# A gated short-convolution layer on one core: sharing buffers between small weight pieces, turning all tokens at the start, and a new load order

## The chip, the core and the metric

The kernel runs on one core of one Trainium2 chip. The metric is the device time of one execution in microseconds (us), which is to be small. The core has four compute engines that run side by side: PE (TensorE, matrix products), DVE (VectorE), ACT (ScalarE) and POOL (GpSimd, hardly used here). SP (SyncE) only issues DMA transfers. Each engine works through its own list of instructions in order; an instruction waits until the semaphores that it names have been reached, and everything behind it on the same engine waits with it.

## What is computed

With 256 tokens of width 2048 and a branch width of 4096, in float32:

```python
h = rmsnorm(x, norm_g)                              # (256, 2048)
mod = silu(c) @ ada_w + ada_b                       # (3 * 2048): shift, scale, gate
h = h * (1 + scale) + shift
b_gate, c_gate, v, g = split(h @ w_in, 4)           # w_in (2048, 16384)
u = causal_depthwise_conv(c_gate * v, conv_w)       # width 3
y = (b_gate * u * silu(g)) @ w_out                  # w_out (4096, 2048)
out = rmsnorm(x + gate * y, final_g)
```

## The kernel before

**Precision.** Each float32 weight tile is split into two parts that PE can take at full rate: ACT casts it to `hi` (L318), DVE subtracts to get `lo` (L323). The modulated tokens are kept turned (channels on the partitions) as `hT`, also in two parts: ACT writes the high part (L310), DVE recomputes the value in `xs` (L311) and writes the low part (L314). Three products replace one: high by high, high weight by low token, low weight by high token. A chunk of 128 channels `k` against 512 columns takes 12 products of 128x256 (`chunk_products`, in that order for each of four column blocks).

**Stages.** (1) The front: load x (four 512 KB pieces) and the shift and scale columns of `ada_w` for channels k = 0 and 1, sum them against silu(c), normalise and turn part of the tokens, form `hT` for k = 0, 1. (2) The stage with tiles `mm_s`: the first half of the columns of `w_in` as 16 parts of 512 columns (4 "chapters" `ch` by 4 quarters `q`). Not all channels of `hT` exist yet, so `plan()` first runs all 16 parts over the few k that are ready, and then comes back to each part as more groups of two k are ready. Sums wait in `acc` tiles. The parts of the plan that matter here are 13 parts over k = 0, 1; three parts over k = 0 to 3; five over k = 2, 3; and then one over k = 2 to 5, the first that uses k = 4. (3) The stage `mm_b`: the second half of the columns, all k at once. (4) `mm_o`: the product with `w_out`, the gate, the last norm.

**ada groups.** The shift and scale for the next two k come from eight pieces of 512 KB (`at`, two loads of 256 KB each, four buffers). DVE multiplies and adds them into `gv` (L410 for the first row block, L412 for the rest). `ada_done` then turns `gv` on PE (`tp_g`, L419), sums over rows on DVE (`gs`, L420), adds the bias (`mod`, L307) and calls `modulate`.

**Order.** A scheduler orders the instructions of each engine by priority and by a simulated time line; the front is pinned to the written order. All loads of weights go through SP's one queue, in order. There are three buffers each for the loaded piece (`raw`), for `hi` and for `lo`, of 2048 columns; a piece over k = 0, 1 fills only half of one. A load waits until DVE has read the buffer's last piece, `hi` and `lo` until PE has. Idle products (`idle`, L243) keep PE busy in the front. The tokens of k = 0 to 3 are scaled and turned in the front (`turn_x`, L287 to L299), those of k = 4 to 15 in three portions after the 4th, 7th and 10th part (`LATER`); `conv_w` is loaded at the start and turned after the 4th part.

Of the kernel before, what the change touches and what calls it, by code (L numbers as in the profile page):

```python
# [8 lines left out]
F32 = mybir.dt.float32  # L9
F32R = mybir.dt.float32r  # L10
AF = mybir.ActivationFunctionType
# [106 lines left out]
def short_conv_layer(ctx: ExitStack, tc: tile.TileContext, x, c, norm_g, ada_w, ada_b, w_in, conv_w, w_out, final_g, out):  # L118
# [73 lines left out]
    xt = [[slot([P, HX], f"x{t}{dh}") for dh in range(2)] for t in range(TT)]  # L192
    for t in range(TT):
        for dh in range(2):
            nc.sync.dma_start(xt[t][dh], x[t * P : (t + 1) * P, dh * HX : (dh + 1) * HX])
    nc.scalar.dma_start(rows1[64:80, :], c.rearrange("o (k p) -> (o k) p", p=P))
# [9 lines left out]
    for n, (j, kk) in enumerate(((0, 4), (4, 4), (8, 4), (12, 2), (14, 1), (15, 1))):  # L206
        at = wpool.tile([P, SLOT], F32, tag=("lo", "hi")[n % 2], name="at0", bufs=3)[:, : kk * 2 * NK0 * P]
        at = at.rearrange("p (k s f) -> p k s f", k=kk, s=2)
        if n == 0:
            wpool.tile([P, 32], F32, tag="line3", name="line3", bufs=1)  # L210
        if j == KT - 1:
            raw0 = raw_tile("raw0")
            first_load(raw0, 0)
        for s in range(2):
            nc.sync.dma_start(at[:, :, s, :], adas[:, j : j + kk, s, 0 : NK0 * P])  # L215
        first_ada.extend(at[:, i] for i in range(kk))
    for k in range(1, NK0):
        first_load(raw0, k)

    ident = const.tile([P, P], F32, tag="ident", name="ident")  # L220
# [15 lines left out]
        return tp  # L236


    tp_idle = psum.tile([P, CT, T], F32, tag="mm", name="tp_idle")

    def idle(n):
        for _ in range(n):
            nc.tensor.transpose(tp_idle[:, 0, 0:P], ident, ident)  # L243


    warm = const.tile([P, 1], F32, tag="warm", name="warm")
    silu = nc.scalar.activation(silu_c, turn(rows1, 64, 80, None), AF.Silu)
    root = nc.scalar.activation(warm, eps_t, AF.Sqrt)
    tc.add_manual_dep(root.ins, silu.ins.name, after, reason="one change of table")
    idle(IDLE[0])  # L250
# [3 lines left out]
    idle(IDLE[1])  # L254


    ssq = const.tile([P, 2, TT], F32, tag="ssq", name="ssq")
# [22 lines left out]
    hl_ = hT[:, :, T : 2 * T]  # L280
    xs = [slot([P, CT, T], f"xs{j}") for j in range(KT // CT)]

    def turn_x(k0, k1, vector=False):

        c0, n = k0 % 8 * P, (k1 - k0) * P
        x0, x1 = (xt[t][k0 // 8][:, c0 : c0 + n] for t in range(TT))
        nc.scalar.activation(x0, x0, AF.Copy, scale=rstd[:, 0:1])  # L287
        if vector:
            nc.vector.tensor_scalar_mul(x1, x1, rstd[:, 1:2])
        else:  # L290
            nc.scalar.activation(x1, x1, AF.Copy, scale=rstd[:, 1:2])
        for i in range(0, k1 - k0, 2):
            tp = psum.tile([P, 2, T], F32, tag="sm", name="tp_x", bufs=2)
            for j in range(2):
                for t, xn in enumerate((x0, x1)):
                    nc.tensor.transpose(tp[:, j, t * P : (t + 1) * P], xn[:, (i + j) * P : (i + j + 1) * P], ident)
            for j in range(2):
                k = k0 + i + j
                nc.scalar.activation(xs[k // CT][:, k % CT], tp[:, j], AF.Copy, scale=gT[:, k : k + 1])  # L299

    mod = const.tile([P, 2, KT], F32, tag="mod", name="mod")

# [10 lines left out]
            )  # L313
            nc.vector.tensor_tensor(out=hl_[:, k], in0=hf, in1=hh_[:, k].bitcast(F32), op=ALU.subtract)  # L314

    def split_hi(raw, n):
        hi = wpool.tile([P, SLOT], F32R, tag="hi", name="hi", bufs=3)
        nc.scalar.copy(hi[:, :n], raw[:, :n])  # L318
        return hi

    def split_lo(raw, n, hi, lo_tag="lo"):
        lo = wpool.tile([P, SLOT], F32R, tag=lo_tag, name="lo", bufs=3)
        nc.vector.tensor_tensor(out=lo[:, :n], in0=raw[:, :n], in1=hi[:, :n].bitcast(F32), op=ALU.subtract)  # L323
        return hi, lo

    def split(raw, n, lo_tag="lo"):

        return split_lo(raw, n, split_hi(raw, n), lo_tag)
# [2 lines left out]

    sums0 = psum.tile([P, 512], F32, tag="sm", name="sum0", bufs=2)
    gv0 = adap.tile([P, 2, 2 * P], F32, tag="gv", name="gv0")[:, :, 0 : NK0 * P]
    turn_x(0, 4)

    def sum0(k, rows, col, halves=(0, 1)):


        for o in range(2 * NK0):
            if o // NK0 in halves:  # L340
                nc.tensor.matmul(
                    sums0[:, o * P : (o + 1) * P], rows[:, o // NK0, (o % NK0) * P : (o % NK0 + 1) * P],
                    col.to_broadcast([P, P]),
                    start=k == min(IDLE_AT) and o == 0, stop=k is None, skip_group_check=True,
                )

    for k in range(KT):
        c_k = silu_c[:, k : k + 1]
        at, gv = first_ada[k], gv0
        if k in IDLE_AT:  # L350
            idle(IDLE_AT[k])
# [13 lines left out]
    idle(IDLE_END)  # L365
    pinned.close()
    with behind(ended):
        for k in range(1, NK0):
            pieces0.append(split_lo(raw0[:, k * CT * P : (k + 1) * CT * P], CT * P, hi0[k - 1]))

# [83 lines left out]
    def part(ch, q, k0, k1, seed):  # L454


        col = q * E + ch * CT * P
        step = SLOT // (CT * P)
        first = k0
        bank = psum.tile([P, CT, T], F32, tag="mm", name="mm_s")  # L460
        if seed:
            nc.scalar.copy(bank, acc[ch, q])
        if pieces0:
            for k in range(NK0):
                chunk_products(bank, *pieces0[k], 0, k, k0, k1, late=True)
            pieces0.clear()
            k0 = NK0
        for s0 in range(k0, k1, step):
            sk = min(step, k1 - s0)
            n = sk * CT * P  # L470
            raw = raw_tile("raw_s")
            nc.sync.dma_start(
                raw[:, :n].rearrange("p (k f) -> p k f", k=sk),
                w_in[0, s0 * P : (s0 + sk) * P, col : col + CT * P].rearrange("(k p) f -> p k f", p=P),
            )
            hi, lo = split(raw, n)
            for i in range(sk):
                chunk_products(bank, hi, lo, i * CT * P, s0 + i, k0, k1, seed)
        keep(ch, q, first, bank, seed)
# [13 lines left out]
            ys.append(slot([P, 2, 2, T], f"y{len(ys)}", F32R))  # L493
            split_y(ys[-1], vq)

    LATER = (4, 7, 10)
    whole = [0] * NCH
    for kind, *step in plan():
        if kind == "ada":
            ada_piece(*step)  # L500
        else:
            ch, k1 = step[0], step[3]
            part(*step)
            if step[2] == 0 and len(acc) in LATER:
                k = 4 + 4 * LATER.index(len(acc))
                with tc.issue_after(last_mm[0].ins), behind(ended):
                    turn_x(k, k + 4)
                    if k == 4:
# [207 lines left out]
```

## Time and profile before

| | |
|---|---|
| median of 3 runs | 925.61 us (924.23 to 926.99) |
| the profiled execution | 925.65 us, of which its profile's span is 923.9 us |
| DVE busy | 614.7 us, 67% of the span |
| ACT busy | 466.2 us, 50% |
| DMA queue with the weights | 226.51 MB, 74.1% of 16 engines' span |
| chain that ended last | PE 90%, DMA 5%, DVE 2% |

The span is counted from the first instruction of the execution to the last. The times of single instructions are from this one execution; those of a PE row overlap, so the cost of a product is read from the distance of starts, not from its own duration. A row of the time line gives the start, the duration of the (merged) row, engine, line, operation, tiles, shape and count, and in brackets the idle time of the engine before it and what ended that.

### The profile page before, as it was taken

To read this page: it belongs to the slowest core of one execution; us is meant where nothing else is said; L and a number is where in the kernel's file an instruction comes from. 1 tells how busy PE (TensorE), PEld (TensorE's weight loads), DVE (VectorE), ACT (ScalarE), POOL (GpSimd) and SP (SyncE) were. 2 spreads that over 40 slices of the span, in tenths; PEclk is the share of its full clock that TensorE was granted. 3 is DMA by queue.
4 is the path that set the end of the run, shared out by engine and by line. 5 is a ranking of instruction groups with operands and counts; after the bars stand their busy time and mean duration, and the time that the engine had idled before them with its cause. 6 is when DMAs were issued, how large, how long until landed. Compare 5 with 4: busy or idle time off the path is not lost.

```text
span 923.9 us, 16438 instructions
## 1 busy us (share of the span) xinstructions
PE 905.0 (98%) x7135; PEld 870.0 (94%) x7135; DVE 614.7 (67%) x593; ACT 466.2 (50%) x417; POOL 0.7 (0%) x6
## 2 busy tenths in 40 slices
PE   7999999999999999999999999999999999999996
PEld 7898999999999999999999999999999988888885
DVE  4798989897686899875554554455454544545882
ACT  3785876655557856644334333443344333443333
POOL 0000000000000000000000000000000000000000
PEclk9999999999999999999999999999999999999999
DMA  9999999999985789676656665666556496566542
GB/s 314 339 362 326 339 367 366 341 373 357 314 294 180 236 297 355 228 241 205 191 185 197 202 192 185 195 204 194 184 185 199 141 343 225 185 208 200 183 136 92
DMA packets 163753, 227.66 MB, mean 246 GB/s; under 512 B 5680, under 2 KB 104160, under 8 KB 163296
## 3 DMA queue, kind: packets, MB, share of 16 engines
q1 hardware_dynamic: 163440, 226.51, 74.1%
q8 instruction: 56, 0.92, 0.4%
q14 instruction: 17, 0.14, 0.0%
q10 hardware_dynamic: 240, 0.09, 0.0%
HBM read 224.49 MB, written 2.10 MB: 245 GB/s over the span
## 4 chain that ended last, share of the span: by engine, by line
PE 90%; DMA 5%; DVE 2%; issue 1%; SPq 1%; ACT 0%; ACTq 0%; DVEq 0%
PE mm_b L429 38%; PE mm_s L429 33%; PE mm_o L615 6%; PE mm_o L614 6%; PE mm_o L613 6%; DMA at<-in_ada_w_dram 3%; DMA raw_s<-in_sc_w_in_dram 1%; DVE lo L323 1%; DVE gv L412 1%; DMA x<-in_x_dram 1%; PE ps_gate L552 0%; SPq L215 0%; PE tp_g L419 0%; ACT hi L318 0%; DVE gv L410 0%
## 5 line engine op out<-in xcount | busy, mean ns | idle before, releaser
L429 PE MATMUL mm_s<-hT,hi 128*128 128x256 f32 x2048 | 351.7, 277 | 1.6 <-ACT hT L310 1.1
L429 PE MATMUL mm_b<-hT,hi 128*128 128x256 f32 x2048 | 348.8, 276 | 0.0
L429 PEld LDWEIGHTS mm_s<-hT,hi 128*128 128x128 f32 x2048 | 309.6, 189 | 2.5 <-ACT hT L310 1.3
L429 PEld LDWEIGHTS mm_b<-hT,hi 128*128 128x128 f32 x2048 | 308.4, 188 | 0.2 <-issue 0.2
L429 PE MATMUL mm_s<-hT,lo 128*128 128x256 f32 x1024 | 283.6, 278 | 4.0 <-DVE lo L323 3.9
L429 PE MATMUL mm_b<-hT,lo 128*128 128x256 f32 x1024 | 282.6, 276 | 0.0
L323 DVE TENSOR_TENSOR lo<-raw,hi 128x2048 fp32r<-128x2048 f32 (+1 forms) x66 | 148.1, 2244 | 134.6 <-ACT hi L318 134.6
L318 ACT CAST hi<-raw 128x2048 fp32r<-128x2048 f32 (+1 forms) x66 | 123.7, 1874 | 209.0 <-PE mm_b L429 153.3
L429 PEld LDWEIGHTS mm_s<-hT,lo 128*128 128x128 f32 x1024 | 192.5, 188 | 5.2 <-DVE lo L323 4.8
L429 PEld LDWEIGHTS mm_b<-hT,lo 128*128 128x128 f32 x1024 | 192.2, 188 | 0.2 <-issue 0.2
L323 DVE TENSOR_TENSOR lo<-raw_s,hi 128x2048 fp32r<-128x2048 f32 (+1 forms) x80 | 147.9, 1850 | 36.0 <-ACT hi L318 35.2
L318 ACT CAST hi<-raw_s 128x2048 fp32r<-128x2048 f32 (+1 forms) x80 | 124.5, 1557 | 72.3 <-PE mm_s L429 49.1
L323 DVE TENSOR_TENSOR lo<-raw_o,hi 128x2048 fp32r<-128x2048 f32 x32 | 73.3, 2291 | 64.9 <-ACT hi L318 64.9
L318 ACT CAST hi<-raw_o 128x2048 fp32r<-128x2048 f32 x32 | 61.0, 1907 | 106.9 <-PE mm_o L615 83.4
L614 PE MATMUL mm_o<-lo,y 128*128 128x512 f32 x256 | 99.7, 391 | 0.0
L613 PE MATMUL mm_o<-hi,y 128*128 128x512 f32 x256 | 99.3, 389 | 0.0
L615 PE MATMUL mm_o<-hi,y 128*128 128x512 f32 x256 | 99.3, 389 | 0.0
L412 DVE SCALAR_TENSOR_TENSOR gv<-at,silu_c,gv 128x512 f32<-128x512 f32 x105 | 78.5, 750 | 5.5 <-DMA at<-in_ada_w_dram 3.9
L450 ACT COPY acc<-mm_s 128x1024 f32<-128x1024 f32 x54 | 54.6, 1012 | 36.8 <-PE mm_s L429 36.8
L614 PEld LDWEIGHTS mm_o<-lo,y 128*128 128x128 f32 x256 | 48.1, 188 | 10.2 <-issue 0.2
L615 PEld LDWEIGHTS mm_o<-hi,y 128*128 128x128 f32 x256 | 48.0, 188 | 10.0 <-issue 0.2
L613 PEld LDWEIGHTS mm_o<-hi,y 128*128 128x128 f32 x256 | 48.0, 188 | 10.0
(90 smaller groups left out, 368.1 us busy)
## 6 DMA issues: line engine op xcount, KB each, us to landing
raw<-in_sc_w_in_dram SPq DMA_DIRECT2D x64, 1024.0 KB, 5.6
raw_s<-in_sc_w_in_dram SPq DMA_DIRECT2D x47, 1024.0 KB, 8.1
raw_o<-in_sc_w_out_dram SPq DMA_DIRECT2D x32, 1024.0 KB, 5.3
at<-in_ada_w_dram SPq DMA_DIRECT2D x114, 256.0 KB, 7.6
raw_s<-in_sc_w_in_dram SPq DMA_DIRECT2D x33, 512.0 KB, 5.8
at_g<-in_ada_w_dram SPq DMA_DIRECT2D x32, 512.0 KB, 7.9
at<-in_ada_w_dram SPq DMA_DIRECT2D x6, 512.0 KB, 8.8
x<-in_x_dram SPq DMA_DIRECT2D x4, 512.0 KB, 6.0
```

Of the source, the lines that this page charges most:

```text
L318: nc.scalar.copy(hi[:, :n], raw[:, :n])
L323: nc.vector.tensor_tensor(out=lo[:, :n], in0=raw[:, :n], in1=hi[:, :n].bitcast(F32), op=ALU.subtract)
L412: nc.vector.scalar_tensor_tensor(out=gv, in0=at4[:, i], scalar=c_k, in1=gv, op0=ALU.mult, op1=ALU.add)
L429: mm = last_mm[0] = nc.tensor.matmul(dst, w, h[:, k], start=begins and left, stop=ends, skip_group_check=True)
L450: nc.scalar.copy(acc[ch, q], bank)
L613: nc.tensor.matmul(po, yh, hi[:, o], start=opens, stop=False, skip_group_check=True)
L614: nc.tensor.matmul(po, yh, lo[:, o], start=False, stop=False, skip_group_check=True)
L615: nc.tensor.matmul(po, yl, hi[:, o], start=False, stop=ct == NCT - 1, skip_group_check=True)
```

## The change

1. Pieces of at most 1024 columns share a buffer set: `places` takes a set (`raw`, `hi`, `lo`), gives its first half to one small piece and its second half to the next one, if that is small too. Three sets thus hold up to six small pieces.
2. All of x is scaled in the front with four instructions of 1024 columns, and turned in four portions `turn_x(0)` to `turn_x(3)`: two ahead of the first ada sums on PE, one at k = 10, one after the last sum. They use the `mm` banks instead of the `sm` ones. The three later portions are gone.
3. The idle products are now six products of 512 columns behind the turn of the vectors; the other places of idle products are gone.
4. Loads: the first piece of `w_in` (`raw0`) comes behind all ada pieces of the front, and `conv_w` after the 10th part, on SP's queue; its turn is after the 14th.
5. `ada_done` gets a higher priority (`later(-LEAD)`, 80), and the splits of the first pieces are kept behind the front.

```diff
-    IDLE = (16, 38)
-    IDLE_AT = {3: 0, 7: 6, 10: 17, 11: 0, 13: 1, 15: 13}
-    IDLE_END = 9
+    LEAD = 80
+    IDLE = 6
+    ON_PE = (3, 7, 10, 11, 13, 15)
...
-    nc.scalar.dma_start(rows2[:, :], conv_w.rearrange("w (k p) -> (w k) p", p=P))
...
-        if j == KT - 1:
-            raw0 = raw_tile("raw0")
-            first_load(raw0, 0)
...
-    for k in range(1, NK0):
+    raw0 = raw_tile("raw0")
+    for k in range(NK0):
         first_load(raw0, k)
...
-            nc.tensor.transpose(tp_idle[:, 0, 0:P], ident, ident)
+            nc.tensor.matmul(tp_idle, ident, ones[:, 0:1].to_broadcast([P, 512]), start=True, stop=True)
...
+    def turn_x(j):
+
+        tp = psum.tile([P, CT, T], F32, tag="mm", name="tp_x")
+        for i in range(CT):
+            for t in range(TT):
+                c0 = (j * CT + i) % 8 * P
+                nc.tensor.transpose(tp[:, i, t * P : (t + 1) * P], xt[t][j // 2][:, c0 : c0 + P], ident)
+        return tp
+
+    def keep_x(j, tp):
+        for i in range(CT):
+            k = j * CT + i
+            nc.scalar.activation(xs[j][:, i], tp[:, i], AF.Copy, scale=gT[:, k : k + 1])
...
+    def places(n):
+
+        if n <= HALF and other_half[0]:
+            tiles, other_half[0] = other_half[0], None
+            return [b[:, HALF:SLOT] for b in tiles]
+        tiles = raw_tile("raw_s"), hi_tile(), lo_tile()
+        other_half[0] = tiles if n <= HALF else None
+        return tiles
...
-    turn_x(0, 4)
+    for dh in range(2):
+        for t in range(TT):
+            nc.scalar.activation(xt[t][dh], xt[t][dh], AF.Copy, scale=rstd[:, t : t + 1])
+    for j in range(2):
+        keep_x(j, turn_x(j))
...
-            ada_done(k0, nk, gv)
+            with later(-LEAD):
+                ada_done(k0, nk, gv)
...
-            raw = raw_tile("raw_s")
+            raw, hi, lo = places(n)
...
-            hi, lo = split(raw, n)
+            with behind(ended if len(acc) < 3 else {}):
+                split_lo(raw, n, split_hi(raw, n, hi), lo=lo)
...
-    LATER = (4, 7, 10)
+    LATER = (10, 14)
```

What this does to the lists of the engines, at three places. The numbers behind a name tell buffers apart and differ between the two programs.

SP, where the loads of the first full-size piece of `w_in` stand (128x4x512, 1 MB; it is the first over four k). Before, the last five kinds of rows up to it:

```order
L472 DMA raw_s_771<-in_sc_w_in_dram 128x2x512
L399 DMA at_985<-in_ada_w_dram 128x2x256 x2
L399 DMA at_1047<-in_ada_w_dram 128x2x256 x2
L399 DMA at_1052<-in_ada_w_dram 128x2x256 x2
L472 DMA raw_s_823<-in_sc_w_in_dram 128x2x512
L472 DMA raw_s_862<-in_sc_w_in_dram 128x4x512
```

Now:

```order
L413 DMA at_576<-in_ada_w_dram 128x2x256 x2
L413 DMA at_645<-in_ada_w_dram 128x2x256 x2
L413 DMA at_683<-in_ada_w_dram 128x2x256 x2
L487 DMA raw_s_651<-in_sc_w_in_dram 128x2x512 x2
L487 DMA raw_s_739<-in_sc_w_in_dram 128x4x512
L413 DMA at_733<-in_ada_w_dram 128x2x256 x2
```

Before, 14 ada pieces had been loaded ahead of it (8 for k = 2, 3 and 6 for k = 4, 5: `at_856` to `at_1052`). Now 8 are, and the first piece for k = 4, 5 (`at_733`) follows it. The w_in pieces ahead of it are the same: `raw0` and twelve small ones.

DVE, where the low part of `hT` for k = 4, 5 is formed (`gs`, `mod`, `xs1`, `hT` belong to k = 4, 5; the `gv` rows are sums for the next group, the `lo` rows splits of weights). Before:

```order
L420 TENSOR_REDUCE gs_1166<-tp_g_1165 128x4
L323 TENSOR_TENSOR lo_1095<-raw_s_1091,hi_1093 128x1024
L412 SCALAR_TENSOR_TENSOR gv_1212<-at_1313,silu_c_129,gv_1212 128x512
L307 TENSOR_TENSOR mod_209<-gs_1166,vec_127 128x2x2
L412 SCALAR_TENSOR_TENSOR gv_1212<-at_1375,silu_c_129,gv_1212 128x512
L311 TENSOR_SCALAR xs1_206<-xs1_206,mod_209 128x256
L412 SCALAR_TENSOR_TENSOR gv_1212<-at_1375,silu_c_129,gv_1212 128x512
L314 TENSOR_TENSOR hT_204<-xs1_206,hT_204 128x256
```

Now:

```order
L425 TENSOR_SCALAR gv_1086<-at_1087,silu_c_128 128x512
L319 TENSOR_TENSOR lo_1129<-raw_s_1127,hi_1128 128x2048
L435 TENSOR_REDUCE gs_1043<-tp_g_1042 128x4
L427 SCALAR_TENSOR_TENSOR gv_1086<-at_1087,silu_c_128,gv_1086 128x512
L297 TENSOR_TENSOR mod_160<-gs_1043,vec_126 128x2x2
L427 SCALAR_TENSOR_TENSOR gv_1086<-at_1182,silu_c_128,gv_1086 128x512 x2
L319 TENSOR_TENSOR lo_1196<-raw_s_1194,hi_1195 128x2048
L427 SCALAR_TENSOR_TENSOR gv_1086<-at_1187,silu_c_128,gv_1086 128x512
L301 TENSOR_SCALAR xs1_157<-xs1_157,mod_160 128x256 x2
L427 SCALAR_TENSOR_TENSOR gv_1086<-at_1187,silu_c_128,gv_1086 128x512
L304 TENSOR_TENSOR hT_155<-xs1_157,hT_155 128x256 x2
```

The rows for k = 4, 5 now stand behind a row that reads the next group's first piece (`at_1087`), and two full-size `lo` rows stand among them instead of one small one. `raw_s_1127` is the piece that the part over k = 2 to 5 uses, and `at_1087` is loaded just behind it. From the second half of `raw0` (not counted) up to and with `at_1087`, SP's list now has 42 units of 512 KB: 12 small pieces, `raw_s_939` and `raw_s_1006` with two each and `raw_s_1094` as 17 small ones, four full-size ones (8 units), and 17 ada pieces.

ACT, at the end of the front. Before:

```order
L318 CAST hi_302<-raw0_113 128x512
L318 CAST hi_306<-raw0_113 128x512
L318 CAST hi_356<-raw_s_354 128x1024
L310 ACTIVATE hT_204<-xs0_205,mod_209 128x256 x2
L287 ACTIVATE x00_84<-x00_84,rstd_193 128x512
```

Now:

```order
L314 CAST hi_243<-raw0_114 128x512
L314 CAST hi_247<-raw0_114 128x512
L300 ACTIVATE hT_155<-xs0_156,mod_160 128x256 x2
L314 CAST hi_300<-raw_s_299 128x1024
L289 ACTIVATE xs3_159<-tp_x_256,vec_126 128x256 x4
```

`hT` for k = 0, 1 (`hT_204`, now `hT_155`) comes ahead of the cast of the second weight piece. From the stage `mm_b` on, the lists of PE, DVE and ACT are the same in both programs.

More of the change, by code (lines that the diff above doesn't have):

```diff
@@ L236, in turn @@
         return tp
-    tp_idle = psum.tile([P, CT, T], F32, tag="mm", name="tp_idle")
     def idle(n):
         for _ in range(n):
-            nc.tensor.transpose(tp_idle[:, 0, 0:P], ident, ident)
+            nc.tensor.matmul(tp_idle, ident, ones[:, 0:1].to_broadcast([P, 512]), start=True, stop=True)
     warm = const.tile([P, 1], F32, tag="warm", name="warm")
+    tp_idle = psum.tile([P, 512], F32, tag="sm", name="tp_idle", bufs=2)
     silu = nc.scalar.activation(silu_c, turn(rows1, 64, 80, None), AF.Silu)
@@ L253, in short_conv_layer @@
     bias = vec[:, KT : 3 * KT].rearrange("p (s k) -> p s k", s=2)
-    idle(IDLE[1])
+    idle(IDLE)
     ssq = const.tile([P, 2, TT], F32, tag="ssq", name="ssq")
@@ L281, in short_conv_layer @@
     xs = [slot([P, CT, T], f"xs{j}") for j in range(KT // CT)]
[L283 to L299, printed above, removed]
+    def turn_x(j):
[9 more added lines that the diff above has]
+            nc.scalar.activation(xs[j][:, i], tp[:, i], AF.Copy, scale=gT[:, k : k + 1])
     mod = const.tile([P, 2, KT], F32, tag="mod", name="mod")
@@ L314, in modulate, with hi_tile, lo_tile, split_hi @@
             nc.vector.tensor_tensor(out=hl_[:, k], in0=hf, in1=hh_[:, k].bitcast(F32), op=ALU.subtract)
-    def split_hi(raw, n):
-        hi = wpool.tile([P, SLOT], F32R, tag="hi", name="hi", bufs=3)
+    def hi_tile():
+        return wpool.tile([P, SLOT], F32R, tag="hi", name="hi", bufs=3)
+    def lo_tile(lo_tag="lo"):
+        return wpool.tile([P, SLOT], F32R, tag=lo_tag, name="lo", bufs=3)
+    def split_hi(raw, n, hi=None):
+        hi = hi_tile() if hi is None else hi
         nc.scalar.copy(hi[:, :n], raw[:, :n])
         return hi
-    def split_lo(raw, n, hi, lo_tag="lo"):
-        lo = wpool.tile([P, SLOT], F32R, tag=lo_tag, name="lo", bufs=3)
+    def split_lo(raw, n, hi, lo_tag="lo", lo=None):
+        lo = lo_tile(lo_tag) if lo is None else lo
         nc.vector.tensor_tensor(out=lo[:, :n], in0=raw[:, :n], in1=hi[:, :n].bitcast(F32), op=ALU.subtract)
         return hi, lo
+    HALF = SLOT // 2
+    other_half = [None]
+    def places(n):
[5 more added lines that the diff above has]
+        return tiles
     def split(raw, n, lo_tag="lo"):
@@ L343, in sum0 @@
                     col.to_broadcast([P, P]),
-                    start=k == min(IDLE_AT) and o == 0, stop=k is None, skip_group_check=True,
+                    start=k == ON_PE[0] and o == 0, stop=k is None, skip_group_check=True,
                 )
@@ L349, in short_conv_layer @@
         at, gv = first_ada[k], gv0
-        if k in IDLE_AT:
-            idle(IDLE_AT[k])
+        if k in ON_PE:
+            if k == 10:
+                keep_x(2, turn_x(2))
             sum0(k, at, c_k, (0,) if k == KT - 1 else (0, 1))
@@ L364, in short_conv_layer @@
     modulate(0, NK0, sums0.rearrange("p (o f) -> p o f", o=2 * NK0)[:, :, 0])
-    idle(IDLE_END)
+    tp_3 = turn_x(3)
     pinned.close()
     with behind(ended):
+        keep_x(3, tp_3)
         for k in range(1, NK0):
@@ L504, in short_conv_layer @@
             if step[2] == 0 and len(acc) in LATER:
-                k = 4 + 4 * LATER.index(len(acc))
                 with tc.issue_after(last_mm[0].ins), behind(ended):
-                    turn_x(k, k + 4)
-                    if k == 4:
+                    if len(acc) == LATER[0]:
+                        nc.sync.dma_start(rows2[:, :], conv_w.rearrange("w (k p) -> (w k) p", p=P))
+                    else:
                         turn(rows2, 0, 96, cw)
```

3 lines of the change are left out of this document (1 added, 2 removed).

## The prediction

> **What bounds the kernel now.** I read the page, then the stages, then the time line of PE.
>
> ```profile
> span 923.9 us, 16438 instructions
> PE 905.0 (98%) x7135; PEld 870.0 (94%) x7135; DVE 614.7 (67%) x593; ACT 466.2 (50%) x417; POOL 0.7 (0%) x6
> ```
>
> PE is nearly always busy, so only two things help: an earlier first product, and fewer holes. The view by stages (length, then busy time and count of PE, PEld, DVE, ACT, POOL, the granted clock, the share of the DMA engines, GB/s) shows where they are:
>
> ```profile
> 0.00:27.60 27.60, 20.81 (x163) 19.47 (x163) 11.71 (x24) 11.19 (x20) 0.70 (x6) 1.00 0.97 314
> 27.60:69.40 41.80, 40.83 (x343) 39.66 (x343) 37.34 (x50) 33.61 (x45) 0.00 (x0) 1.00 1.05 354
> 69.40:80.00 10.60, 8.30 (x58) 8.30 (x59) 10.41 (x14) 3.98 (x5) 0.00 (x0) 0.84 1.07 359
> 80.00:108.20 28.20, 26.98 (x238) 26.74 (x237) 25.23 (x33) 23.68 (x24) 0.00 (x0) 1.00 0.97 314
> 108.20:250.00 141.80, 141.80 (x1253) 141.80 (x1253) 121.42 (x129) 88.99 (x73) 0.00 (x0) 1.00 1.03 354
> ```
>
> Behind 108.2 PE has no hole, so whatever the change gains must be gained ahead of that. There the DMA engines are full and DVE is busy about 90% of the time: three resources are close to each other. The time line of PE has these places:
>
> ```profile
> 27.60 0.74 PE L429 MATMUL mm_s<-hT,hi 128*128 128x256 f32 x4 [1.07 <-ACT hT L310]
> 59.28 1.03 PE L296 MATMUL tp_x<-ident,x 128*128 128x128 f32 x8
> 60.07 0.48 PE L429 MATMUL mm_s<-hT,hi 128*128 128x256 f32 x2
> 71.70 0.39 PE L429 MATMUL mm_s<-hT,lo 128*128 128x256 f32 x1 [2.31 <-DVE lo L323]
> 105.72 0.39 PE L429 MATMUL mm_s<-hT,lo 128*128 128x256 f32 x1 [1.22 <-DVE lo L323]
> ```
>
> and the stages around the hole at 69.4 show what followed it:
>
> ```profile
> 70.00:72.00 2.00, 0.30 (x2) 0.30 (x3) 2.00 (x2) 1.20 (x2) 0.00 (x0) 1.00 1.09 349
> 72.00:74.00 2.00, 2.00 (x16) 2.00 (x15) 2.00 (x6) 1.23 (x1) 0.00 (x0) 0.81 1.08 362
> 74.00:76.00 2.00, 2.00 (x12) 2.00 (x11) 2.00 (x2) 0.00 (x0) 0.00 (x0) 0.50 1.06 388
> 76.00:78.00 2.00, 2.00 (x16) 2.00 (x16) 1.97 (x4) 0.00 (x0) 0.00 (x0) 0.84 1.07 370
> ```
>
> A hole of 2.31 us cost the clock as well: 2 x (0.19 + 0.50 + 0.16) = 1.7 us of PE's work. The 1.22 us hole at 104.5 did not (the clock of 80 to 108.2 is 1.00).
>
> **How long the products take by themselves.** The chain of waits gives the rate of products, and the landings of four loads:
>
> ```profile
> 20.05 5.84 DMA raw_s<-in_sc_w_in_dram
> 59.52 9.15 DMA at<-in_ada_w_dram
> 94.82 6.73 DMA at<-in_ada_w_dram
> 251.76 62.61 PE mm_s L429 x552
> 314.38 1.72 PE ps_gate L552 x4
> ```
>
> A product costs 62.61 / 552 = 0.1134 us. Up to the first use of k = 4 the plan has 13 x 24 + 3 x 48 + 5 x 24 + 24 = 600 of them: 68.0 us. The hole at 105.72 is before the third product of the part over k = 2 to 5 (high by high, high by low, then `lo`), so the product that first needs the low `hT` of k = 4, its 26th, came 23 x 0.1134 = 2.6 later, at 108.3. From 27.6 that is 80.7 us: 68.0 of products, 3 x 0.79 for tokens (59.28 to 60.07), about 1.4 for three `tp_g` and the turn of conv_w, and 8.9 of holes and slow clock. These 2.4 and 8.9 us, and what the first product gains, are all that can be won: at most about 13 us.
>
> **The change, part by part.**
>
> *The first product.* The rows that set it:
>
> ```profile
> 4.22 3.67 PE L243 MATMUL tp_idle<-ident 128*128 128x128 f32 x16
> 8.53 4.37 PE L243 MATMUL tp_idle<-ident 128*128 128x128 f32 x38
> 24.49 1.05 PE L341 MATMUL sum<-ones,gv 128*128 128x128 f32 x8
> 23.36 0.62 ACT L318 CAST hi<-raw 128x512 fp32r<-128x512 f32 x1 [7.25 <-DMA raw<-in_sc_w_in_dram]
> 26.00 1.04 ACT L318 CAST hi<-raw_s 128x1024 fp32r<-128x1024 f32 x1 [0.66 <-DMA raw_s<-in_sc_w_in_dram]
> 26.95 1.09 ACT L310 ACTIVATE hT<-xs,mod 128x256 fp32r<-128x256 f32 x2
> 25.58 0.16 DVE L307 TENSOR_TENSOR mod<-sum,vec 128x4 f32<-128x4 f32 x1 [0.49 <-PE sum L341]
> ```
>
> `mod` was ready at 25.74, but ACT was at the cast of the next piece until 26.95. The new order on ACT removes that: 27.6 - 1.2 = 26.4. The last ada piece no longer waits for a quarter MB of `raw0`: 256 KB at 354 GB/s is 0.7 us, so 25.7 at best. The added work of the front (four scalings of about 1 us and twelve copies of 1/4 of a portion) lies in ACT's 7.25 us of idle time. On PE the start is slower: the 16 idle turns ran at 0.229 us each and the 38 behind them at 0.115, so the first 3.7 us of work went at half rate. Those 16 are gone, so now the six wide products start cold, at 8.5. I have no row of them; `ps_gate` is the nearest, a float32 product of 512 columns in two records of 0.43, so 0.86. Cold for 3.9 us and then warm they end at 15.6, cold throughout at 18.8. Behind them come about 9 us of turns and sums (7.2 before between 13.3 and 25.5 without the idle turns, and 16 more turns of 0.11), then 0.9 as from 25.54 to `hT`'s first half: 25.5, or 28.7 at worst. I take 25.8 for the first product.
>
> *The tokens.* The three portions leave the stream: 2.4 us less on PE, and six scalings and twelve copies less on ACT between 28 and 62. The turn of conv_w stays, later; its load (0.4 us of SP's time, between ada pieces queued far ahead) has nobody waiting for it until the chapters are whole.
>
> *Shared buffers and load order.* Before, six ada pieces of the group k = 4, 5 were loaded ahead of the first full-size piece; now none is. At 1.5 us each this piece comes 9 us earlier, while PE comes to it about 6 us earlier (68 - 62), so the 2.3 us hole and its clock loss go; what is late next is its `lo`, ready 0.6 us ahead of PE. A set is free again only when both halves are read: the fourth pair waits for PE's end with `raw_s_299`, at 25.8 + 0.4 + 3 x 2.72 = 34.4, and lands about 41, so the loads hide it. Of small stalls I keep 0.4 us near the first products, where nothing changes on DVE.
>
> *The group k = 4, 5.* This is the price of that order: its sums now end late. DVE's rows for the chain (the distance of starts is what counts):
>
> ```profile
> 69.36 2.29 DVE L323 TENSOR_TENSOR lo<-raw_s,hi 128x2048 fp32r<-128x2048 f32 x1
> 71.56 0.75 DVE L412 SCALAR_TENSOR_TENSOR gv<-at,silu_c,gv 128x512 f32<-128x512 f32 x1
> 72.23 0.73 DVE L311 TENSOR_SCALAR xs<-xs,mod 128x256 f32<-128x256 f32 x2
> 72.87 0.76 DVE L314 TENSOR_TENSOR hT<-xs,hT 128x256 fp32r<-128x256 f32 x2
> 77.07 0.49 DVE L410 TENSOR_SCALAR gv<-at,silu_c 128x512 f32<-128x512 f32 x1
> 77.59 2.33 DVE L412 SCALAR_TENSOR_TENSOR gv<-at,silu_c,gv 128x512 f32<-128x512 f32 x3
> 85.91 0.68 DVE L420 TENSOR_REDUCE gs<-tp_g 128x4 f32<-128x512 f32 x1
> 86.51 1.21 DVE L323 TENSOR_TENSOR lo<-raw_s,hi 128x1024 fp32r<-128x1024 f32 x1
> ```
>
> So a full `lo` takes 2.20, a `gv` 0.67 (0.78 behind its like), the pair `xs` 0.64, a first `gv` 0.52, `gs` 0.60, `mod` 0.16. The order of DVE (shown with the change) puts eleven rows from the `gv` that reads `at_1087` to `hT`: 0.52 + 2.20 + 0.60 + 0.67 + 0.16 + 1.45 + 2.20 + 0.67 + 0.64 + 0.67 + 0.4 = 10.2 us. It starts when `at_1087` lands. The load that landed at 20.05 + 5.84 = 25.89 was the first piece behind `raw0`; the `at` that landed at 68.67 was the 28th unit of 512 KB behind that: 1.53 each, where 354 GB/s gives 1.48. `at_1087` is now the 41st behind the first piece, which itself lands about 0.2 earlier (48 KB of conv_w gone): 25.7 + 41 x 1.48 to 1.53 = 86.4 to 88.4, mid 87.4. Hence the low part of k = 4 is ready at 97.6. PE is there at 25.8 + 0.4 + 68.0 + 1.0 (two `tp_g`, conv_w) + 0.1 = 95.3. PE thus waits 2.3 us, as long as at 69.4, and I take the same 1.7 us for the clock.
>
> The page "TensorE: Matmul & The Clock Gate" of the Trainium skill (HAM oscillation) warns only of idle gaps above about 3.4 us. The rows at 72 to 78 differ, half rate behind 2.31 us, and the measurement decides; by the page the sum would be 1.7 us lower.
>
> *Early ada turns.* The higher priority costs nothing as long as `gv` is whole when PE comes to `tp_g`.
>
> **The sum.** From the low part of k = 4 to the end there were 923.9 - 108.3 = 815.6 us; one `tp_g` (0.4) of the three is still to come. 97.6 + 815.6 + 0.4 + 1.7 = 915.3 for the span. The profiled execution was 925.65, 1.75 more than its span, and the median 925.61: **917.1 us**, or 916.1 to 918.1 with the two paces of the loads. Note that the first product's time drops out: any value below 28.1 only changes how long PE waits at k = 4.
>
> **Rivals.**
>
> 1. *The wait at k = 4 comes, but the clock holds.* 1.7 less: 915.4. For it: the 1.22 us hole cost no clock, and 2.3 is just at what did. The Trainium skill's 3.4 us, in the section named above, would have it so. Chance 0.17.
> 2. *No wait at k = 4*, because DVE or the loads run ahead. PE alone: 95.3 + 815.6 + 0.4 + 1.75 = 913.1. Against it: DVE was 37.34 of 41.80 us busy, so it can't make up much. Chance 0.13.
> 3. *The loads slip.* From 68.67 to the landing at 94.82 + 6.73 = 101.55 there were 21 units, 1.57 each, with SP waiting for buffers. At that pace throughout, `at_1087` lands at 25.7 + 41 x 1.57 = 90.1, 2.7 later: 919.8; sets that come free only in pairs speak for it. Chance 0.13.
> 4. *No change.* The loads decide behind 108 too (share 1.03), and PE, ahead of them by 10 us, waits there for what it gained: 925.6. Against it: a group of two k holds 16 x 24 products, 43.5 us of PE, but 4 MB of ada and 8 MB of w_in, 24 units x 1.5 = 36 us of loads, and on DVE 16 `gv` and 16 small `lo` (1.14), 31 us, and some 3 more. Chance 0.07.
> 5. *Slower: PE stands at each `tp_g`* (L435), which the priority puts in its list ahead of products that it could do. A stop as at 69.4 costs 2.3 + 1.7 = 4.0; five later groups have one: 917.1 + 20 = 937. It passes 928.4 from three groups on, that is if a group's last `gv` trails PE by over 2.3 us each time. The 43.5 against 36 us speaks against a repetition. Chance 0.05.
>
> The forecast itself has 0.45. A measurement of this kernel can tell about 0.3%, 2.8 us, from no change: faster is the forecast and rivals 1 to 3, 0.87 (a little of rival 3 reaches 922.8); same 0.08; slower 0.05. The range: 912.5, below rival 2, to 921.0, above rival 3; it leaves out rivals 4 and 5.
>
> **What would show it.** Right: the first product at 25 to 27; no `tp_x` behind it; no hole near 69; one hole of about 2 us near 95 that `hT` of DVE ends, with a clock near 0.5 behind it; none behind 100. The product rate unchanged. Wrong: holes ended by `gs`, `gv` or PE's own `tp_g`; DMA share under 1 between 30 and 90; or PE waiting for `lo` behind 108.

## The result and the profile after

| | before | after |
|---|---|---|
| median | 924.92 us (923.42 to 926.99, 4 runs) | 913.78 us (913.44 to 914.15, 4 runs) |
| the profiled execution | 925.65 us, span 923.9 | 913.68 us, span 911.9 |

The change makes the kernel 1.2% faster: the ratio of the times is 0.9876, with a 95% interval of 0.986 to 0.9893. In the medians this is 11.1 us, where 8.5 were forecast; the likeliest case of the forecast was not the one that came, though. PE's own share, from the page of the changed kernel:

```profile
span 911.9 us, 16239 instructions
PE 895.7 (98%) x7047; PEld 858.5 (94%) x7047; DVE 616.2 (68%) x593; ACT 464.6 (51%) x413; POOL 0.7 (0%) x6
```

The span is 12.0 us shorter, PE's busy time 9.3 us, DVE's and ACT's are what they were. The stages of the changed kernel, in the columns of the view of before:

```profile
26.00:69.40 43.40, 43.15 (x376) 42.66 (x375) 38.82 (x49) 31.52 (x35) 0.00 (x0) 1.00 1.07 369
69.40:80.00 10.60, 10.60 (x96) 10.60 (x95) 9.49 (x10) 7.85 (x8) 0.00 (x0) 1.00 1.05 349
80.00:108.20 28.20, 28.14 (x247) 27.95 (x247) 26.61 (x31) 23.94 (x23) 0.00 (x0) 1.00 1.06 365
108.20:250.00 141.80, 141.80 (x1253) 141.80 (x1251) 126.66 (x142) 86.00 (x72) 0.00 (x0) 1.00 1.03 349
```

Where before showed 8.30 of 10.60 us at a clock of 0.84 there is now no gap and a clock of 1.00. In the first three stages together PE stands for 0.3 us, in the last for nothing. PE's time line in the front (each of the six idle products makes two records), and the rows that begin the stream:

```profile
8.81 7.07 PE L237 MATMUL tp_idle<-ones,ident 128*128 128x512 f32 x12
15.73 1.91 PE L283 MATMUL tp_x<-ident,x 128*128 128x128 f32 x16
20.13 3.29 PE L353 MATMUL sum<-silu_c,at 128*128 128x128 f32 x28
23.26 1.05 PE L353 MATMUL sum<-ones,gv 128*128 128x128 f32 x8
24.15 1.03 PE L283 MATMUL tp_x<-ident,x 128*128 128x128 f32 x8
25.32 0.72 PE L444 MATMUL mm_s<-hT,hi 128*128 128x256 f32 x4
40.20 0.39 PE L444 MATMUL mm_s<-hT,lo 128*128 128x256 f32 x1 [0.25 <-DVE lo L319]
```

The first product lies at 25.32 (27.60 before), and the one row behind it with a wait over 0.2 us up to 110 is that at 40.20. The 12.0 us of the span are thus 2.28 at the start, 3 x 0.79 = 2.4 of tokens that no longer stand in the stream, and the rest, 7.3 us. The four holes of before and the slow clock make 6.1 of these (worked out with the shared sets alone, below); the other 1.2 us lie in gaps of PE too small to be told apart here.

### The profile page after: what moved, and what is told of

It reads as the page before. It is cut to its first block, busy times and chain, and to the rows that moved or that the text cites. A ratio compares the mean times of both kernels' runs of the same rounds, so it can differ in the third digit from the quotient of the medians.

```text
span 911.9 us, 16239 instructions
## 1 busy us (share of the span) xinstructions
PE 895.7 (98%) x7047; PEld 858.5 (94%) x7047; DVE 616.2 (68%) x593; ACT 464.6 (51%) x413; POOL 0.7 (0%) x6
## 4 chain that ended last, share of the span: by engine, by line
PE 94%; DMA 3%; ACT 1%; SPq 1%; DVE 0%; issue 0%; ACTq 0%
PE mm_b L444 38%; PE mm_s L444 36%; PE mm_o L631 6%; PE mm_o L629 6%; PE mm_o L630 6%; DMA raw_s<-in_sc_w_in_dram 2%; DMA at<-in_ada_w_dram 1%; SPq L210 1%; DMA x<-in_x_dram 1%; ACT hi L314 0%; PE ps_gate L568 0%; PE tp_g L434 0%; ACT acc L465 0%; DVE lo L319 0%; ACT hT L300 0%; SPq L413 0%
## 5 line engine op out<-in xcount | busy, mean ns | idle before, releaser
L319 DVE TENSOR_TENSOR lo<-raw_s,hi 128x2048 fp32r<-128x2048 f32 (+1 forms) x80 | 147.6, 1850 | 25.6 <-ACT hi L314 24.6
L630 PEld LDWEIGHTS mm_o<-lo,y 128*128 128x128 f32 x256 | 48.1, 188 | 10.2 <-issue 0.2
L631 PEld LDWEIGHTS mm_o<-hi,y 128*128 128x128 f32 x256 | 48.0, 188 | 10.2 <-issue 0.2
```

The lines of the kernel that those rows point to most:

```text
L630: nc.tensor.matmul(po, yh, lo[:, o], start=False, stop=False, skip_group_check=True)
L631: nc.tensor.matmul(po, yl, hi[:, o], start=False, stop=ct == NCT - 1, skip_group_check=True)
```

## The experiments

The theory, once the result was known: three separate gains (start, tokens, holes), the last from the shared sets, which bring the first full-size piece of `w_in` earlier; and the wait that I had forecast at k = 4 was hidden because PE's list is not in the order of the plan there. Rivals: the holes went because ACT, DVE and PE were rid of the tokens; the higher priority of the ada turns did it; there never was anything to wait for at k = 4. Each ratio below is to executions of the kernel before that ran beside that run; their medians were 925.68 us for the first four runs on record (own sets, old priority, tokens, plan's order), 923.91 for the next four and 924.21 for the last three.

### Every small piece with a set of its own

```diff
-        if n <= HALF and other_half[0]:
+        if False:
```

> The changed kernel, but each small piece gets a set of buffers of its own again, so 15 pieces of ada are loaded ahead of the first full-size piece of w_in (8 in the changed kernel, 14 before). Theory (the shared sets closed the hole at 69 by bringing that piece earlier): PE comes there about 4.7 us earlier than before (2.3 of the first product, 2.4 of tokens) and the piece lands about 1.3 us later (one ada piece more, 1.5, less 0.2), so the hole is 2.3 + 4.7 + 1.3 = 8.3 us, with 1.7 for the clock: 913.8 + 10.0 = 923.8 us, within 922 to 925. The low part of hT for k = 4 comes before PE needs it. Rival (the hole went because the tokens left the stream and relieved ACT and DVE): no hole over 1 us, 914 to 916 us.

Measured: 924.75 us (923.01 to 927.5, 11 runs), ratio to before 0.9995 (0.9981 to 1.0009). The whole gain is gone, though tokens and front are those of the changed kernel. PE's rows with the longest waits up to 72, and the stages behind the last:

```profile
37.48 0.39 PE L444 MATMUL mm_s<-hT,lo 128*128 128x256 f32 x1 [0.76 <-DVE lo L319]
59.12 0.39 PE L444 MATMUL mm_s<-hT,lo 128*128 128x256 f32 x1 [0.75 <-DVE lo L319]
68.80 0.50 PE L444 MATMUL mm_s<-hT,hi 128*128 128x256 f32 x2 [0.76 <-ACT hi L314]
71.33 0.39 PE L444 MATMUL mm_s<-hT,lo 128*128 128x256 f32 x1 [2.03 <-DVE lo L319]
```

```profile
72.00:74.00 2.00, 2.00 (x15) 2.00 (x14) 1.48 (x2) 0.97 (x1) 0.00 (x0) 0.72 1.05 368
74.00:76.00 2.00, 2.00 (x11) 2.00 (x10) 1.95 (x2) 0.77 (x1) 0.00 (x0) 0.50 1.10 355
76.00:78.00 2.00, 2.00 (x17) 2.00 (x17) 1.27 (x2) 1.13 (x1) 0.00 (x0) 0.92 1.06 368
```

The sum that I gave, 923.8, was about right, but in part by luck, as its shape was not: instead of one hole of 8.3 us there is a row of waits from 36 on, and one of 2.0 us at the place of the old one, with the slow clock behind it, 2 x (0.28 + 0.50 + 0.08) = 1.7 us. PE, which starts earlier than before and has no tokens in its stream, meets each piece earlier, and so waits for several of them. All waits up to 110 make 6.5 us (the four above and 0.46, 0.44, 0.37 and 0.91), the clock 1.7, and the first product lies at 26.79, 1.5 us later than in the changed kernel, as the idle products took longer: 9.7 of the 11.5 us between the two spans. The reason is in DVE's rows for the first full-size `lo`, here, and then in the changed kernel:

```profile
68.99 2.28 DVE L319 TENSOR_TENSOR lo<-raw_s,hi 128x2048 fp32r<-128x2048 f32 x1
```

```profile
57.96 2.29 DVE L319 TENSOR_TENSOR lo<-raw_s,hi 128x2048 fp32r<-128x2048 f32 x1
```

It is 11 us earlier with the shared sets (69.36 in the kernel before). The rival of the tokens falls.

### The kernel before with the shared sets alone

`places` as in the diff of the change, put into the kernel before with its use, and nothing else:

```diff
-            raw = raw_tile("raw_s")
+            raw, hi, lo = places(n)
...
-            hi, lo = split(raw, n)
+            split_lo(raw, n, split_hi(raw, n, hi), lo=lo)
```

> The kernel before with the shared sets of buffers alone: 9 ada pieces instead of 14 are loaded ahead of the first full-size piece. Theory (the shared sets alone close the holes): the front and the tokens cost what they did, and of the 8.9 us of holes and slow clock about 7.3 go, as between the two traces: 925.6 - 7.3 = 918.3 us, at least the 4.0 us of the hole at 69 with its clock: 921.6 at most. Rival (the sets bring nothing while ACT has the tokens to turn in the stream): 925 us.

Measured: 919.08 us (918.96 to 919.32, 6 runs), ratio 0.9938 (0.992 to 0.9956). This is 0.8 us more than the 918.3 expected; it is 5.8 less than the 924.92 of before, and 4.8 less than the 923.91 of the executions beside it. The kernel before has four waits behind its first product up to 110, the two in the prediction and these, on PE's time line:

```profile
37.63 0.51 PE L429 MATMUL mm_s<-hT,hi 128*128 128x256 f32 x2 [0.49 <-ACT hi L318]
47.57 0.39 PE L429 MATMUL mm_s<-hT,lo 128*128 128x256 f32 x1 [0.40 <-DVE lo L323]
```

With the shared sets the first product is where it was, no row with a wait follows it up to 110, and the first full-size `lo` starts at 62.27 (PE's row, then DVE's):

```profile
27.55 0.72 PE L447 MATMUL mm_s<-hT,hi 128*128 128x256 f32 x4 [0.81 <-ACT hT L310]
```

```profile
62.27 2.29 DVE L329 TENSOR_TENSOR lo<-raw_s,hi 128x2048 fp32r<-128x2048 f32 x1 [0.92 <-ACT hi L324]
```

So the sets alone close all four holes: 0.49 + 0.40 + 2.31 + 1.22 = 4.4 us, and 1.7 of clock, 6.1. The 11 executions of before beside this run fall into two groups: six took 923.27 to 923.91 us with a mean granted clock of 0.998 or 0.999, five took 925.17 to 928.71 with 0.995 or 0.996. So the clock seems to be lost in some executions only, and against the six that keep it the sets bring about 4.6 us, close to the 4.4 of the holes. The remaining 919.08 - 913.78 = 5.3 us fit the start and the tokens, 2.3 + 2.4 on the time lines, and some 0.6 of smaller things; no run changes the start alone.

### Tokens in the stream again

The changed kernel with `turn_x` of before, its three portions after the 4th, 7th and 10th part, and the rest as changed:

```diff
-    for j in range(2):
-        keep_x(j, turn_x(j))
+    turn_x(0, 4)
...
-    LATER = (10, 14)
+    LATER = (4, 7, 10, 14)
```

> The changed kernel with the tokens of k = 4 to 15 scaled and turned in three portions in the stream, as before. Theory (a portion costs PE 0.8 us and nothing else): 3 x 0.8 = 2.4 us more, 916.2 us, with no hole at 69, and a first product at 25.3 or up to 0.5 earlier. Rival (the portions on ACT and the sm banks cause the holes): holes of several us between 27 and 108, 920 us or more. Second rival (the portions fill time in which PE would wait): 914 us. The list of PE is in the plan's order at k = 4 in this kernel, so up to 1 us of wait near 98 may come on top of each.

Measured: 917.51 us (917.42 to 919.46, 5 runs), ratio 0.9918 (0.9903 to 0.9934), 3.7 us more than the changed kernel; 2.4 were expected. PE's rows behind the first product and one of the three portions, then ACT's that explain them:

```profile
24.90 0.74 PE L440 MATMUL mm_s<-hT,hi 128*128 128x256 f32 x4 [1.40 <-ACT hT L304]
29.39 0.50 PE L440 MATMUL mm_s<-hT,hi 128*128 128x256 f32 x2 [0.99 <-ACT hi L318]
30.65 0.39 PE L440 MATMUL mm_s<-hT,lo 128*128 128x256 f32 x1 [0.76 <-DVE lo L323]
38.71 1.04 PE L290 MATMUL tp_x<-ident,x 128*128 128x128 f32 x8
```

```profile
25.24 0.71 ACT L281 ACTIVATE x<-x,rstd 128x512 f32<-128x512 f32 x1
...
27.70 0.71 ACT L281 ACTIVATE x<-x,rstd 128x512 f32<-128x512 f32 x1
28.31 1.03 ACT L318 CAST hi<-raw_s 128x1024 fp32r<-128x1024 f32 x1
```

The first product comes 0.4 us earlier, and 1.75 us of waits follow: ACT is at five scalings of tokens from 25.24 to 28.3, ahead of the casts of which PE awaits the first. 2.4 + 1.75 - 0.4 = 3.75. No hole comes back at 69, and none comes near 98. A portion costs PE what I took, and its scalings cost more than nothing when they stand between two casts.

### The old priority for the ada turns

```diff
-            with later(-LEAD):
-                ada_done(k0, nk, gv)
+            ada_done(k0, nk, gv)
```

> The changed kernel with the turn of the ada sums at its old priority. Theory (priority has no part in the gain): 913.8 us, within 0.5. Rival (the higher priority brought the low part of hT for k = 4 early enough): the hT of k = 4 is formed later, PE waits near 98, 915 to 918 us.

Measured: 914.1 us (913.88 to 914.71, 4 runs), ratio 0.9875 (0.986 to 0.989). The row that writes the low `hT` of k = 4 starts at 96.65, 0.3 us later than in the changed kernel, and PE has no wait there. The priority has no part in the gain that these times can tell.

### PE held to the order of the plan

PE's list in the changed kernel is not in the order of the plan at k = 4. The scheduler had put 25 products of the next part, over a piece that was ready, between the first product of k = 4 and the one that needs the low `hT`. (The lists with the old priority and with the shared sets alone have the same 25 there; those of the kernel before and with own sets are in the plan's order.) The order of PE in the changed program (`mm_s_1125` and `hi_1128` are the bank and the weights of the part over k = 2 to 5, `mm_s_1192` and `hi_1195` those of the next part):

```
436 L444 MATMUL mm_s_1125<-hT_155,hi_1128 128x256
437 L444 MATMUL mm_s_1192<-hT_155,hi_1195 128x256 x2
438 L444 MATMUL mm_s_1192<-hT_155,lo_1196 128x256
...
453 L444 MATMUL mm_s_1192<-hT_155,hi_1195 128x256
454 L444 MATMUL mm_s_1125<-hT_155,hi_1128 128x256
455 L444 MATMUL mm_s_1125<-hT_155,lo_1129 128x256
```

PE's time line there:

```profile
95.61 0.84 PE L444 MATMUL mm_s<-hT,hi 128*128 128x256 f32 x3
96.28 0.28 PE L444 MATMUL mm_s<-hT,lo 128*128 128x256 f32 x1
...
98.69 0.28 PE L444 MATMUL mm_s<-hT,lo 128*128 128x256 f32 x1
98.80 0.39 PE L444 MATMUL mm_s<-hT,hi 128*128 128x256 f32 x2
```

The first row begins with the first product of k = 4; the second product of the last row is the one that needs the low part. DVE's rows at the two ends of the chain in the prediction:

```profile
86.57 0.49 DVE L425 TENSOR_SCALAR gv<-at,silu_c 128x512 f32<-128x512 f32 x1 [0.50 <-DMA at<-in_ada_w_dram]
...
95.07 0.73 DVE L301 TENSOR_SCALAR xs<-xs,mod 128x256 f32<-128x256 f32 x2
95.72 0.74 DVE L427 SCALAR_TENSOR_TENSOR gv<-at,silu_c,gv 128x512 f32<-128x512 f32 x1
96.38 0.75 DVE L304 TENSOR_TENSOR hT<-xs,hT 128x256 fp32r<-128x256 f32 x2
```

The low part of k = 4 is the first half of the last row, so ready at about 96.38 + 0.4 = 96.8: 1.1 us behind 95.7, where the plan's order would have PE, and 2 us ahead of where PE needs it. The experiment takes the 25 products away from there:

```diff
-        mm = last_mm[0] = nc.tensor.matmul(dst, w, h[:, k], start=begins and left, stop=ends, skip_group_check=True)
+        mm = nc.tensor.matmul(dst, w, h[:, k], start=begins and left, stop=ends, skip_group_check=True)
+        if last_mm[0] is not None:
+            tc.add_manual_dep(mm.ins, last_mm[0].ins.name, after, reason="the plan's order")
+        last_mm[0] = mm
```

> The changed kernel with PE's products held to the order of the plan, so that the product that needs the low part of hT for k = 4 stands right behind the first of its part and not 25 products later. Theory (the wait that I forecast was hidden by the scheduler's order): PE is at that product at 95.7 and the low part comes at 96.8, a wait of 1.1 us with no loss of clock, 913.8 + 1.1 = 914.9 us; with the loss of clock 916.6. Rival (the order is of no account, DVE runs ahead): 913.8 us, no wait. Second rival (the scheduler's order hid other waits too): further holes, 917 us or more.

Measured: 914.65 us (914.15 to 915.25, 4 runs), ratio 0.988 (0.9865 to 0.9896). PE's rows:

```profile
96.19 0.28 PE L444 MATMUL mm_s<-hT,hi 128*128 128x256 f32 x1
97.44 0.39 PE L444 MATMUL mm_s<-hT,hi 128*128 128x256 f32 x1 [0.97 <-DVE hT L304]
```

The wait is there, 1.25 us from start to start, that is 1.1 more than the 0.11 of a product, and it ends with `hT`; the median is 0.9 us higher. No clock went. So what hid the wait was the order, and what it hid was small.

### The same wait, made as long as forecast

```diff
-            nc.vector.tensor_tensor(out=hl_[:, k], in0=hf, in1=hh_[:, k].bitcast(F32), op=ALU.subtract)
+            for _ in range(2 if k == 4 else 1): nc.vector.tensor_tensor(out=hl_[:, k], in0=hf, in1=hh_[:, k].bitcast(F32), op=ALU.subtract)
```

on top of the plan's order. DVE does the same subtraction a second time, which PE has to await.

> The kernel with PE in the order of the plan, and on DVE the subtraction that gives the low hT of k = 4 done a second time, with a gv of the next group ahead of it: 0.67 + 0.33 + 0.33 = 1.35 us later, so the wait of 1.13 us at 96 becomes 2.5 us. My forecast took half the clock for some 3.4 us behind such a hole (1.7 us of work). Theory (a hole of 2.5 us costs the clock, as those of 2.31 and 2.19 us did, one of 1.1 to 1.25 does not): 914.65 + 1.35 + 1.7 = 917.7 us, with a granted clock of 0.5 in one stretch of 2 us some 3 to 6 us behind the hole. Rival (the clock went for another reason, the many small holes ahead of those two, which are missing here): 916.0 us and a clock of 1.00.

Measured: 917.92 us (916.19 to 918.51, 6 runs), ratio 0.9922 (0.9905 to 0.994). PE's rows, and the stages behind:

```profile
95.52 0.28 PE L444 MATMUL mm_s<-hT,hi 128*128 128x256 f32 x1
98.11 0.38 PE L444 MATMUL mm_s<-hT,hi 128*128 128x256 f32 x1 [2.31 <-DVE hT L304]
```

```profile
98.00:100.00 2.00, 1.90 (x10) 1.90 (x11) 2.00 (x3) 0.57 (x1) 0.00 (x0) 0.60 1.08 371
100.00:102.00 2.00, 2.00 (x12) 2.00 (x12) 1.97 (x3) 0.00 (x0) 0.00 (x0) 0.55 1.06 372
102.00:104.00 2.00, 2.00 (x20) 2.00 (x19) 1.11 (x2) 1.46 (x1) 0.00 (x0) 1.00 1.08 354
```

A gap of 2.31 us, the same as at 69 in the kernel before, and the clock is 0.60 and 0.55 in the two stretches behind it: 2 x (0.40 + 0.45) = 1.7 us. No row with a wait over 0.2 us stood ahead of it here, so that rival falls. The lowest of the six executions, 916.19, has a mean granted clock of 0.997, the other five, 917.6 to 918.51, of 0.995 or 0.996: the theory's sum without the clock is 914.65 + 1.35 = 916.0. The page "TensorE: Matmul & The Clock Gate" of the Trainium skill (HAM oscillation) warns of idle gaps above about 3.4 us; the rows here and in the kernel before show the loss behind 2.31 us, the first kernel of these experiments behind 2.03, and none behind 0.97 or 1.22.

### The front

Two edits of the changed kernel. The first quarter of `raw0` is loaded ahead of the last ada piece again:

```diff
+        if j == KT - 1:
+            raw0 = raw_tile("raw0")
+            first_load(raw0, 0)
...
-    raw0 = raw_tile("raw0")
-    for k in range(NK0):
+    for k in range(1, NK0):
```

> The changed kernel with the first quarter of raw0 (256 KB) loaded ahead of the last ada piece of the front again, as before. Theory (the last ada piece sets the first product, so 256 KB at 354 GB/s are 0.7 us): 913.8 + 0.7 = 914.5 us. Rival (PE's turns and sums of the front set it, as they run without a pause from 15.7 to 25.2): 913.8 us.

And there are no idle products:

```diff
-    IDLE = 6
+    IDLE = 0
```

> The changed kernel without the six idle products. Theory (they are worth the clock that they warm): the turns and sums from 13.7 on, when the first scaled x is there, run at half rate for 3.9 us as the first idle turns did before, and lose 1.9 us, but start 2.0 us earlier than behind the idle products (15.7): 913.8 us, within 0.7. Rival (the front of PE is the bound and the start at half rate is not made up): 915.7 us. Second rival (the products only stand in the way): 912.5 us.

Measured: 913.83 us (913.59 to 914.1, 5 runs), ratio 0.988 (0.9862 to 0.9898), and 914.3 us (913.75 to 914.49, 5 runs), ratio 0.9885 (0.9867 to 0.9902). The load order costs nothing, so its rival holds here: in the profile of the changed kernel PE runs its turns and sums without a pause from 15.73 to 25.2. Without idle products the kernel is some 0.5 us slower, hardly above the spread, and its first product lies at 26.45. Then `IDLE = 4` and `IDLE = 3`, with the changed kernel once more beside them:

> The changed kernel itself once more, beside the two that follow. Every theory: 913.8 us, within 0.5. Its first product lay at 25.3 in the first profile and, in kernels with the same front, at 25.6 to 26.8; if the start of the clock after the idle products sets it (they took 7.07, 7.66 and 8.23 us), it falls in that stretch again, as far behind their end as before (9.6 us).

> The changed kernel with four idle products instead of six. Theory (behind the idle products PE runs turns and sums without a pause, so their end sets the first product until DVE's last gv, at 23.1, does): the idle products end about 14 to 15, PE then waits for gv, the first product lies at 25.3 each time and not at 25.3 to 26.8, and the time is 0.5 us lower: 913.3. Rival (the clock is not warm after four, and the turns run at half rate): 914.3 us, as without any.

> The changed kernel with three idle products. Theory: they end at 12.7 or a little later, before the first scaled x is there at 13.6, so PE pauses for about 1 us; the front is then set by DVE's gv as with four, 913.3 us. Rival (too few for the clock): 914.3 us.

Measured: 913.68 (913.33 to 914.16, 4 runs; ratio 0.9885, 0.987 to 0.9899) with six, 913.81 (913.48 to 914.11, 4 runs; ratio 0.9886, 0.9871 to 0.99) with four, 913.68 (913.5 to 913.72, 4 runs; ratio 0.9884, 0.9868 to 0.9901) with three. My 913.3 did not come, nor did the rival's 914.3. PE's rows with three:

```profile
8.61 5.49 PE L237 MATMUL tp_idle<-ones,ident 128*128 128x512 f32 x6
22.31 1.23 PE L353 MATMUL sum<-ones,gv 128*128 128x128 f32 x8
24.93 0.74 PE L444 MATMUL mm_s<-hT,hi 128*128 128x256 f32 x4 [0.51 <-ACT hT L300]
```

PE now waits for `hT` again, the first product is 0.4 us earlier than in the changed kernel's first profile (25.59 in its second), and nothing of that is left at the end. What takes it back was not tried; in this profile the starts of PE's products show two gaps of 0.3 to 0.4 us between 26 and 29 that the changed kernel hasn't. Nor does the start decide much: first products at 24.93 (three), 25.32 and 25.59 (six), 25.37 (four), 26.26 (the other load order) and 26.45 (none) go with 913.5, 913.68 and 913.59, 913.76, 914.02 and 914.32 us in the same executions, so that, as far as single executions tell, of 1.5 us some 0.8 are left at the end. No version here beats the changed kernel by more than the spread.

## Why the forecast was right, and where not

- *The first product.* Right within the stretch of 25 to 27, and by luck within half a microsecond: 25.8 forecast, 25.3 and 25.6 measured, but 26.1, 26.5 and 26.8 in three kernels with the same front (old priority, plan's order, own sets). The idle products ended at about 15.8 where 15.6 was worked out from `ps_gate`; the half rate, taken as 3.9 us, lasted 3.4 in that execution and 5.2 to 6.0 in these three. The term for `raw0` (0.7) played no part, since PE's own front was the later one.
- *The tokens.* Right: 2.4 us. Taking them back costs 3.7, as their scalings on ACT then also delay casts.
- *The holes.* Right, and the largest gain: with the shared sets undone the time is that of before again, and alone they bring 4.8 to 5.8.
- *The loads and DVE up to `hT` of k = 4.* Nearly right: DVE took `at_1087` at 86.57 (87.4 forecast, 87.4 - 86.57 = 0.8), and from there to the low part it was the 10.2 us of the sum, 96.8 in place of 97.6.
- *The wait at k = 4.* **This step failed**: "PE is there at 25.8 + 0.4 + 68.0 + 1.0 + 0.1 = 95.3. PE thus waits 2.3 us". PE did come to k = 4 at 95.61, but I had carried over from the kernel before that the product with the low `hT` comes right behind the first of k = 4. In the new list 25 others stand between the two, 25 x 0.1134 = 2.8 us of work. Held to the plan's order, PE waits 1.1 us and the time is 914.65. The 2.3 us were thus 1.2 too long as well, 0.8 of it from the loads and 0.3 from PE.
- *The clock behind it.* The term of 1.7 us was right as a mechanism and had no occasion: stretched to 2.31 us, the wait costs it in five of six executions, median 917.92 us.

What came was rival 2 (913.1, where 913.78 was measured), and the stated range held because it took that rival in. It came for another reason than the one I named: not DVE or the loads ran ahead, PE had other work in its list. What tells it is the order of PE in the new program at the first use of k = 4; I read the lists of SP, DVE and ACT there, and not PE's. Rival 1's wait is the one in plan order. Rivals 3, 4 and 5 left no trace: the loads kept their pace, PE doesn't wait for them behind 108, and no `tp_g` stops it.

## What to carry to other kernels

When buffers are handed out by the piece, a small piece holds up a large one: letting two small pieces share a set moved the split of the first large piece 7 us forward by itself (69.36 to 62.27) and 11 us with the rest of the change, and closed every hole of the stream. Starting an engine earlier is worth only what its later inputs allow; with the old sets the whole gain of start and tokens went into waiting. And before a wait is forecast for a new order, count the products that stand in the new list between the arrival and the one that needs the late operand.

## What the runs showed of the hardware

In the profiled executions gaps of 1.22 us (the kernel before) and 1.40 (ahead of the first product, with the tokens in the stream) cost no clock, and gaps of 2.03 and 2.31 did. Between 1.40 and 2.03 nothing was measured. The loss was the same each time, whether smaller gaps stood ahead or not: one stretch of 3.41 us at half the clock, 1.7 us of work. It began 1.5 us behind the end of the gap in the kernel before, 1.6 with own sets and 0.3 with the stretched wait:

```profile
73.23:76.64 3.41, 3.41 (x19) 3.41 (x18) 3.41 (x5) 0.00 (x0) 0.00 (x0) 0.50 1.05 380
72.90:76.31 3.41, 3.41 (x18) 3.41 (x18) 3.05 (x3) 1.15 (x2) 0.00 (x0) 0.50 1.09 358
98.38:101.79 3.41, 3.41 (x18) 3.41 (x18) 3.38 (x4) 0.19 (x1) 0.00 (x0) 0.50 1.06 373
```

The three kernels with such a gap also scatter: 923.01 to 927.5 with sets of their own, 916.19 to 918.51 with the stretched wait and 923.42 to 926.99 before, against 913.44 to 914.15 for the changed kernel. The mean granted clock of each execution goes with it, most clearly in the two groups named with the shared sets alone and in the stretched wait, so the same gap seems to cost the clock in some executions and not in others; why is not shown. It is not the only source of scatter: tokens in the stream scatter by 2 us at 0.997 to 0.999, without such a gap in their profile.

The half rate at the start is no fixed time. The idle products began at 8.81 in the changed kernel, and twelve records took 7.07 us; with the other load order at 8.65, and they took 8.23:

```profile
8.65 8.23 PE L239 MATMUL tp_idle<-ones,ident 128*128 128x512 f32 x12
```

From start to start a warm record takes 0.43 us and a cold one 0.855. In the changed kernel the record that starts at 11.54 is the first to take less than a cold one, 0.74, so the half rate ended about 12.16, 3.4 us behind the first start; with the other load order it was the record at 13.93, with 0.63, so 14.33 and 5.7 us. The edit is not what decides: the second profile of the changed kernel gives 4.1 us, four idle products 2.8, the plan's order 6.0, and the six records with three idle products, 5.49 us, were all cold. The page "TensorE: Matmul & The Clock Gate" of the Trainium skill (Part 1) has the clock open about 4 us into sustained products, 0.5 us either way, after a busy window of about 3.4 us that runs free of the program. The 3.4 and 4.1 us are near that; 2.8, 5.7 and 6.0 lie outside the scatter that it gives. The granted clock, the column ahead of the last two in the view by stages, reads 1.00 in this part of the changed kernel, so it shows the slow clock behind a gap and not the one at the start:

```profile
10.00:12.00 2.00, 2.00 (x4) 0.84 (x3) 1.76 (x7) 0.00 (x0) 0.00 (x0) 1.00 1.09 362
```
